# Four of the first modulation's sixteen maps taken as row sums on VectorE, the other twelve left on TensorE, and the first loads in a new order

## The chip, the cores and the metric

One core of one Trainium2 chip runs the whole program. The metric is device time in microseconds (us) of one execution. Engines are named as in the profile: PE is TensorE, PEld its weight loads, DVE VectorE, ACT ScalarE, POOL GpSimd, SP SyncE, which here only issues transfers.

## The reference, cut to what matters

A trunk of two layers works on 256 context tokens and 1024 latent tokens, 1024 features wide; layer 0 mixes tokens by a Conformer convolution module, layer 1 by grouped-query attention, and each is followed by a SwiGLU FFN. Only the first steps of layer 0 are touched by the change:

```python
silu_c, silu_cc = jax.nn.silu(c), jax.nn.silu(c_ctx)          # 1024 values each
mod_x = (silu_c  @ w_mod[i] + b_mod[i])[:, None, :]           # w_mod[i] is 1024 x 6144
mod_c =  silu_cc @ w_mod[i] + b_mod[i]
sh_x, sc_x, g_x, shf_x, scf_x, gf_x = jnp.split(mod_x, 6, axis=-1)
hx = rmsnorm(x,   norm_g[i, 0]) * (1.0 + sc_x) + sh_x
hc = rmsnorm(ctx, norm_g[i, 0]) * (1.0 + sc_c) + sh_c
yx, yc = conv_module(hx, ...), conv_module(hc, ...)           # begins with h @ w_pw1 (1024 x 2048)
```

So nothing of the first large matmul (pw1) can be completed before the first 2048 columns of the modulation, shift (sh) and scale (sc), are there: 16 blocks of 128 features, called maps here, numbers 0 to 7 for sh and 8 to 15 for sc.

## The kernel before, in words

Activations lie feature by token: 8 blocks k of 128 features on the partitions. The tokens are cut into three pieces: C (the 256 context tokens), L and R (512 latent tokens each). Every large matmul is made of three passes over a high and a low half of each operand (lines 450, 451 and 452 in `pw1`: high weights by high data, high by low, low by high).

`build` writes the work down in an order, and a scheduler turns it into one fixed queue of instructions for each engine, after data dependences and priorities. Each engine then works its queue strictly in order and waits by semaphores. The steps of the beginning are:

- `load_x` asks for the activations of a piece in four transfers (256 KB each for C, 512 KB for L and R), `load_map(i)` for one map of 512 KB, in the order map 0, map 8, map 1, map 9, and so on, into ten buffers. "The n-th map" below is the n-th in this order, counted from 0. All are issued by SP; a transfer is issued only once the one eight before it has landed.
- `mod_pe` computes one map on PE: eight matmuls (line 241) against both conditions at once give two rows of 128 values, ACT copies them (line 244), PE turns them upright (line 246), and ACT adds the bias (line 248). Two maps, sh and sc of the same block k, then let DVE make the scale column of block k (line 1095 before, 1128 after).
- `norm_in` is the RMS norm of a piece. ACT squares the eight blocks (lines 385 and 388), DVE adds them up (389), PE sums over the partitions (363), DVE takes the reciprocal root in some 12 dependent small instructions (341 to 368), PE spreads it (377). Then each block is applied: DVE multiplies (397), ACT adds the shift and rounds to the high half (402), DVE makes the low half (403). gC, gL and gR are the three pieces' norms, advanced in turn by `next`.
- `wload` loads a weight block of 512 KB into one of the two buffers wr0 and wr1 and splits it into a high half on ACT (143) and a low half on DVE (147). The first two blocks of pw1 are loaded in this way while the norms run.
- `cond_row` loads both conditions as one row repeated on all 128 partitions (1 MB, line 252) and takes their SiLU there (253). It serves `mod_dve`, which computes the later maps 16 to 39 on DVE during pw1: one dot product of a transposed map against a condition is one DVE instruction of 128 by 1024 and a small one that reads the accumulator (line 271).

PE's queue ends the beginning with pw1's block 0 on C and L, then the sums (363) and the spreading (377) of R's norm, then the second half of L and everything that follows.

Of the kernel before, what the change touches and what calls it, by code (L numbers as in the profile page):

```python
# [12 lines left out]
ALU = mybir.AluOpType  # L13
# [4 lines left out]
KT = D // P  # L18
# [36 lines left out]
class Kern:  # L55
# [1001 lines left out]
    def build(self):  # L1057
        nc, a, c = self.nc, self.a, None
        self.consts()
        c = self.c  # L1060
# [4 lines left out]
        cr = hr[:, TOK + nv:TOK + nv + 2048].rearrange("p (s d) -> p s d", s=2)  # L1065
        xs = {"C": hr[:, :KT * CTX].rearrange("p (k n) -> p k n", k=KT), "L": self.T("T6", [P, KT, 512])}

        def load_x(b):
            for q in range(0, KT, 2):
                nc.sync.dma_start(xs[b][:, q:q + 2, :], a["xT"][:, q:q + 2, PIECES[b][0]:PIECES[b][1]])  # L1070
        load_x("C")
        gC = self.norm_in(0, None, (None, "T1", "T1"), *PIECES["C"], hs["C"], xt=xs["C"])
        gL = self.norm_in(0, None, (None, "T2", "T3"), *PIECES["L"], hs["L"], xt=xs["L"])
        self.set_banks(mm=[0, 1, 2, 3], md=[4, 6], st=[4, 5, 6, 7])
# [4 lines left out]
        raws = [self.T(t, [P, 4, 1024]) for t in ("T4", "T5")] + [self.T("KB", [P, 2, 1024])]  # L1079
        raws = [raws[i][:, j] for j in range(4) for i in range(3) if j < raws[i].shape[1]]  # L1080

        def load_map(i):
            if i < 2 * KT:
                nc.sync.dma_start(raws[i % len(raws)], a["wmod"][i % 2 * KT + i // 2])
        for i in range(len(raws)):
            if i == 6:
                load_x("L")
            load_map(i)
        self.lo_dve = 1.0
        for k in range(KT):  # L1090
            for i in (2 * k, 2 * k + 1):
                self.mod_pe(i % 2 * KT + k, raws[i % len(raws)])
                load_map(i + len(raws))
            for s in range(2):
                nc.vector.scalar_tensor_tensor(out=self.col[0][s][0][:, k:k + 1], in0=self.mod[0][s][:, 8 + k:9 + k],
                                               scalar=1.0, in1=c["ng"][:, 0, 0, k:k + 1], op0=ALU.add, op1=ALU.mult)
            if k == 0:
                for _ in range(KT + 1):
                    next(gC)
            if k == 2:  # L1100
                for _ in range(KT + 1):
                    next(gL)
            next(gC)
            if k >= 2:
                next(gL)
            if k == 3:
                self.pre += [self.wload(a["pw1"][0]), self.wload(a["pw1"][KT])]
                xs["R"] = self.T("HS", [P, KT, 512])
                load_x("R")
                gR = self.norm_in(0, None, (None, "T4", "T5"), *PIECES["R"], hs["R"], xt=xs["R"])  # L1110
                self.cond_row(cr)
            if k > 3:
                for _ in range(3 if k < 6 else 2):
                    next(gR)
# [370 lines left out]
```

## Time and profile before

| | |
|---|---|
| median of 3 runs | 2964.86 us (2963.69 to 2965.74) |
| the profiled execution's own time | 2965.05 us |
| its span, first to last instruction | 2963.1 us |
| PE busy in the span | 2881.2 us, 97% |
| DVE busy | 1918.5 us, 65% |
| ACT busy | 1199.2 us, 40% |
| mean granted TensorE clock | 0.988 |

All times in the trace count from the first instruction of the span; 1.95 us of the execution's time lie outside it. A busy PE of 97% is an average over 3 ms: the change concerns only the first 70 us, which have to be read by themselves.

### The profile page before, as it was taken

The numbers are of one execution on the slowest core, as the hardware profiler recorded it, in microseconds if no ns is written. First come the engines' busy times: TensorE is split into PE (matmuls) and PEld (weight loads), VectorE is DVE, ScalarE is ACT, GpSimd is POOL, SyncE is SP. The second block draws the span as 40 slices with busy tenths as digits, with TensorE's granted clock in tenths as the row PEclk, the third lists the DMA queues.
The fourth block names the chain that finished last, engine by engine and source line by source line (L and its number), as shares of the span: only waits on it lengthen the run. The fifth ranks groups of instructions, "written<-read, shape, count | busy, mean of one in ns | idle before, by whom it ended". The sixth has DMA issues, their size and how long they took to land.

```text
span 2963.1 us, 38878 instructions
## 1 busy us (share of the span) xinstructions
PE 2881.2 (97%) x14914; PEld 2397.3 (81%) x14914; DVE 1918.5 (65%) x3340; ACT 1199.2 (40%) x1976; POOL 225.4 (8%) x381
## 2 busy tenths in 40 slices
PE   8999989999999999999999999989999999999997
PEld 5888877888888888888878777767777778888886
DVE  6887787847556368333577899786666657543335
ACT  5222265522222134222345788645555543332222
POOL 0000001011122011000011111100000000000000
PEclk9999999999999999999999999999999999999998
DMA  6443434334355234333355211322213143442332
GB/s 246 131 126 97 121 131 152 126 121 135 117 171 182 60 119 157 100 97 96 129 173 164 61 49 45 107 79 82 80 58 87 58 142 103 146 142 93 97 95 64
DMA packets 132138, 336.35 MB, mean 114 GB/s; under 512 B 31472, under 2 KB 53008, under 8 KB 130800
## 3 DMA queue, kind: packets, MB, share of 16 engines
q1 hardware_dynamic: 78624, 222.59, 23.3%
q0 software_dynamic: 29408, 103.83, 10.8%
q10 hardware_dynamic: 23920, 7.44, 1.1%
q8 instruction: 117, 1.92, 0.3%
q14 instruction: 69, 0.57, 0.1%
HBM read 289.50 MB, written 38.93 MB: 111 GB/s over the span
## 4 chain that ended last, share of the span: by engine, by line
PE 88%; DVE 7%; issue 2%; DMA 2%; ACT 1%; ACTq 0%; POOL 0%; SPq 0%; DVEq 0%; POOLq 0%
PE ps L171 21%; PE ps L172 21%; PE ps L173 21%; PE ps L982 4%; PE ps L1000 4%; PE ps L1006 2%; PE ps L1007 2%; PE ps L450 2%; PE ps L452 2%; PE ps L451 2%; PE ps L661 1%; PE ps L183 1%; PE ps L528 1%; PE ps L182 1%; PE ps L184 1%
## 5 line engine op out<-in xcount | busy, mean ns | idle before, releaser
L171 PE MATMUL ps<-T,wh 128*128 128x512 f32 (+1 forms) x2032 | 768.5, 378 | 0.5 <-DVE sm L804 0.4
L173 PE MATMUL ps<-T,wl 128*128 128x512 f32 (+1 forms) x2032 | 765.6, 377 | 3.0 <-DVE wl L147 3.0
L172 PE MATMUL ps<-T,wh 128*128 128x512 f32 (+1 forms) x1984 | 746.1, 376 | 0.0
L143 ACT CAST wh<-wr 128x1024 fp32r<-128x1024 f32 x285 | 299.3, 1050 | 737.4 <-PE ps L172 549.6
L147 DVE TENSOR_TENSOR wl<-wr,wh 128x1024 fp32r<-128x1024 f32 x285 | 348.4, 1223 | 291.4 <-ACT wh L143 286.6
L173 PEld LDWEIGHTS ps<-T,wl 128*128 128x128 f32 x2032 | 384.4, 189 | 73.1 <-DVE wl L147 3.7
L171 PEld LDWEIGHTS ps<-T,wh 128*128 128x128 f32 x2032 | 384.3, 189 | 69.8 <-ACT T L1345 1.7
L172 PEld LDWEIGHTS ps<-T,wh 128*128 128x128 f32 x1984 | 375.2, 189 | 66.4 <-DVE T L163 0.7
L172 PE MATMUL ps<-HS,wh 128*128 128x512 f32 (+1 forms) x768 | 297.7, 388 | 0.0
L1004 DVE TENSOR_TENSOR T<-ps,T 128x512 fp32r<-128x512 f32 x320 | 216.8, 687 | 108.1 <-ACT T L1003 107.3
L171 PE MATMUL ps<-HS,wh 128*128 128x512 f32 (+1 forms) x720 | 277.7, 388 | 0.0
L173 PE MATMUL ps<-HS,wl 128*128 128x512 f32 (+1 forms) x720 | 277.7, 386 | 0.0
L1003 ACT CAST T<-ps 128x512 fp32r<-128x512 f32 x320 | 185.9, 585 | 190.8 <-PE ps L1000 177.1
L1000 PE MATMUL ps<-cst,T 128*128 128x128 f32 x1100 | 189.3, 274 | 3.1 <-DVE T L1004 3.1
L988 DVE TENSOR_SCALAR_CACHE_REDUCE T<-ps,rq 128x1280 f32<-128x1280 f32 x110 | 170.0, 1546 | 28.0 <-PE ps L982 22.1
L835 DVE TENSOR_TENSOR T<-ps,T 128x512 f32<-128x512 f32 (+1 forms) x168 | 110.3, 662 | 116.2 <-PE ps L173 115.7
L1000 PEld LDWEIGHTS ps<-cst,T 128*128 128x128 f32 x1100 | 132.8, 141 | 49.3 <-DVE T L1004 30.6
L810 DVE TENSOR_TENSOR sm<-sm,ps 128x256 f32<-128x256 f32 (+1 forms) x88 | 54.5, 619 | 181.6 <-PE ps L173 181.5
L172 PEld LDWEIGHTS ps<-HS,wh 128*128 128x128 f32 x768 | 144.8, 188 | 27.6 <-DVE HS L163 0.2
L990 ACT ACTIVATE T<-T,mn 128x1280 f32<-128x1280 f32 x110 | 150.3, 1366 | 38.8 <-DVE T L988 38.4
L173 PEld LDWEIGHTS ps<-HS,wl 128*128 128x128 f32 x720 | 135.3, 188 | 26.9
L171 PEld LDWEIGHTS ps<-HS,wh 128*128 128x128 f32 x720 | 135.0, 188 | 26.2 <-ACT HS L160 0.8
(280 smaller groups left out, 4635.6 us busy)
## 6 DMA issues: line engine op xcount, KB each, us to landing
wr<-in_w SPq DMA_DIRECT2D x220, 512.0 KB, 3.5
q<-in_w SPq DMA_DIRECT2D x44, 512.0 KB, 3.4
wr<-in_pw SPq DMA_DIRECT2D x35, 512.0 KB, 3.5
HR<-in_wmodT POOLq DMA_DIRECT2D x56, 256.0 KB, 3.9
q<-in_wmodT POOLq DMA_DIRECT2D x56, 256.0 KB, 3.9
q<-qsd POOLq DMA_DIRECT2D x32, 256.0 KB, 3.3
wr<-in_wo SPq DMA_DIRECT2D x16, 512.0 KB, 3.5
qsd<-T POOLq DMA_DIRECT2D x14, 512.0 KB, 3.6
```

Of the source, the lines that this page charges most:

```text
L143: nc.scalar.copy(hi, raw)
L147: nc.vector.tensor_tensor(lo, raw, hi.bitcast(F32), op=ALU.subtract)
L171: nc.tensor.matmul(out[:, :n], lhsT=wh, rhs=xh, start=k == 0, stop=False)
L172: nc.tensor.matmul(out[:, :n], lhsT=wh, rhs=xl, start=False, stop=False)
L173: nc.tensor.matmul(out[:, :n], lhsT=wl, rhs=xh, start=False, stop=k == nk - 1)
L835: nc.vector.tensor_tensor(yd, out[:, :c1 - c0], yd, op=ALU.add)
L982: nc.tensor.matmul(sc[:, k0:k0 + w], lhsT=q[:, h, :], rhs=kt[:, p * TOK + k0:p * TOK + k0 + w], start=p == 0, stop=p == 1)
L988: nc.vector.tensor_scalar(out=pt, in0=sc, scalar1=rq[:, h:h + 1], scalar2=None, op0=ALU.mult, op1=ALU.min, accum_out=mn)
L990: nc.scalar.activation(pt, pt, AF.Exp, bias=mn, scale=-1.0, accum_out=sums[:, 0, h:h + 1])
L1000: nc.tensor.transpose(tp[:, h * P:(h + 1) * P], Ps[h][:, j * P:(j + 1) * P], c["ident"])
L1003: nc.scalar.copy(ph, tp)
L1004: nc.vector.tensor_tensor(pl, tp, ph.bitcast(F32), op=ALU.subtract)
```

## The change

Maps 6, 14, 7 and 15 (the sh and sc of blocks 6 and 7) leave PE. Their transposed form (`wmodT`, 512 KB each as well) is loaded, and DVE forms their eight dot products (`by_row`, line 1092) and adds the biases (line 1126). For this the conditions' row is loaded and its SiLU taken early instead of beside R. The first two maps are asked for ahead of the context tokens. Maps 6 and 15 go through the spare buffer q, maps 14 and 7 through wr1 and wr0, the buffers that pw1's first two weight blocks use next. The bytes that are loaded are the same.

```diff
-        load_x("C")
...
         def load_map(i):
-            if i < 2 * KT:
-                nc.sync.dma_start(raws[i % len(raws)], a["wmod"][i % 2 * KT + i // 2])
-        for i in range(len(raws)):
-            if i == 6:
-                load_x("L")
+            nc.sync.dma_start(raws[i % len(raws)], a["wmod"][i % 2 * KT + i // 2])
+
+        rows = [(f, self.raw() if i else self.room()) for i, f in enumerate((6, 14, 7))]
+        junk = self.ps[:, 2:4].rearrange("p a b -> p (a b)")
+
+        def load_row(f, raw):
+            nc.sync.dma_start(raw, a["wmodT"][0, f])
+
+        def by_row(f, raw):
+            for s in range(2):
+                nc.vector.tensor_tensor_reduce(out=junk, in0=raw, in1=cr[:, s, :], scale=1.0, scalar=0.0,
+                                               op0=ALU.mult, op1=ALU.add, accum_out=self.mod[0][s][:, f:f + 1])
+        for i in range(2):
             load_map(i)
+        load_x("C")
+        for i in (2, 3):
+            load_map(i)
+        self.cond_row(cr)
+        load_row(*rows[0])
+        for i in (4, 5):
+            load_map(i)
+        load_x("L")
+        load_map(6)
+        load_row(*rows[1])
+        load_map(7)
+        load_row(*rows[2])
+        for i in (8, 9):
+            load_map(i)
+        for row in rows:
+            by_row(*row)
+        rows.append((15, self.room()))
         self.lo_dve = 1.0
         for k in range(KT):
             for i in (2 * k, 2 * k + 1):
-                self.mod_pe(i % 2 * KT + k, raws[i % len(raws)])
-                load_map(i + len(raws))
+                if i < 12:
+                    self.mod_pe(i % 2 * KT + k, raws[i % len(raws)])
+                if i < 2:
+                    load_map(i + len(raws))
+                if i == 1:
+                    load_row(*rows[3])
+                    by_row(*rows[3])
+                    for s in range(2):
+                        for f in (6, 14):
+                            m = self.mod[0][s][:, f:f + 2]
+                            nc.vector.tensor_tensor(m, m, c["bmod"][:, 0, f:f + 2], op=ALU.add)
...
                 gR = self.norm_in(0, None, (None, "T4", "T5"), *PIECES["R"], hs["R"], xt=xs["R"])
-                self.cond_row(cr)
```

DVE's queue at the root of L's norm, before: sum (nv), root (nq, nh, nr) and the first application to L (sb<-T6) stand nearly together.

```order
L368 TENSOR_SCALAR nv_296<-ps_72 128x4
L341 TENSOR_SCALAR nq_304<-nv_296 128x4
L345 TENSOR_SCALAR nh_303<-nv_296 128x4
L343 TENSOR_SCALAR nr_302<-nq_304 128x4
L347 TENSOR_TENSOR nq_304<-nr_302 128x4
L403 SCALAR_TENSOR_TENSOR T1_204<-sb_321,mod01_102,T1_204 128x256
L348 TENSOR_TENSOR nq_304<-nq_304,nh_303 128x4
```

The same place after the change; the instructions that read wr1 and wr0 are the dot products of maps 14 and 7.

```order
L1092 ISA ps_72,mod00_101<-wr1_74,HR_105 128x1024
L1092 ISA mod00_101 128x1
L368 TENSOR_SCALAR nv_312<-ps_72 128x4
L1092 ISA ps_72,mod01_102<-wr1_74,HR_105 128x1024
L1092 ISA mod01_102 128x1
L341 TENSOR_SCALAR nq_320<-nv_312 128x4
L345 TENSOR_SCALAR nh_319<-nv_312 128x4
L343 TENSOR_SCALAR nr_318<-nq_320 128x4
L347 TENSOR_TENSOR nq_320<-nr_318 128x4
L348 TENSOR_TENSOR nq_320<-nq_320,nh_319 128x4
L349 SCALAR_TENSOR_TENSOR nr_318<-nq_320,nr_318 128x4
L1092 ISA ps_72,mod00_101<-wr0_73,HR_105 128x1024
```

Two dots of map 14 stand ahead of the root and two of map 7 inside it (the second of these a few rows on); before, none did.

PE's queue where L's root is spread (line 377), before: the sixth and seventh map are just done, and eight maps are still to come.

```order
L246 MATMUL ps_72<-cst_75,sm_339 128x2
L377 MATMUL ps_72<-cst_75,nr_302 128x128 x4
L246 MATMUL ps_72<-cst_75,sm_352 128x2
L241 MATMUL ps_72<-T4_113,cs_99 2x128 x8
L241 MATMUL ps_72<-T5_114,cs_99 2x128 x8
```

After the change, the same place in PE's queue:

```order
L246 MATMUL ps_72<-cst_75,sm_368 128x2
L241 MATMUL ps_72<-T4_109,cs_99 2x128 x8
L377 MATMUL ps_72<-cst_75,nr_318 128x128 x4
L241 MATMUL ps_72<-T5_110,cs_99 2x128 x8
L246 MATMUL ps_72<-cst_75,sm_406 128x2
L241 MATMUL ps_72<-T4_109,cs_99 2x128 x5
L246 MATMUL ps_72<-cst_75,sm_419 128x2
L241 MATMUL ps_72<-T4_109,cs_99 2x128 x3
L241 MATMUL ps_72<-T5_110,cs_99 2x128 x8
```

The spreading now stands between map 8 and map 9, and maps 9, 10 and 11, the last three on PE, are queued behind it.

DVE's queue after the scale columns (line 1095, 1128) of block 4, before: C and L are applied and the two low halves of pw1's weights follow (L147).

```order
L1095 SCALAR_TENSOR_TENSOR col010_112<-mod01_102,cst_75 128x1
L397 SCALAR_TENSOR_TENSOR sb_412<-HR_105,col010_112,ps_72 128x256
L397 SCALAR_TENSOR_TENSOR sb_416<-T6_106,col000_111,ps_72 128x512
L403 SCALAR_TENSOR_TENSOR T1_204<-sb_412,mod01_102,T1_204 128x256
L403 SCALAR_TENSOR_TENSOR T3_326<-sb_416,mod00_101,T2_325 128x512
```

After the change, the dots of map 15 (buffer q) stand there:

```order
L1128 SCALAR_TENSOR_TENSOR col010_108<-mod01_102,cst_75 128x1
L1092 ISA ps_72,mod00_101<-q_142,HR_105 128x1024
L1092 ISA mod00_101 128x1
L397 SCALAR_TENSOR_TENSOR sb_426<-HR_105,col010_108,ps_72 128x256
L1092 ISA ps_72,mod01_102<-q_142,HR_105 128x1024
L1092 ISA mod01_102 128x1
L1126 TENSOR_TENSOR mod00_101<-mod00_101,cst_75 128x2
L147 TENSOR_TENSOR wl_384<-wr1_74,wh_383 128x1024
```

pw1's first low half now follows the dots of map 15. Up to the spreading of R's root (line 377 again) PE's queue holds the same pw1 matmuls in both kernels, 48 of 256 columns and 18 of 512.

## Rows read from the trace of the kernel before

**Rows 1.** Busy time of each engine by stretch of the span: stretch, its length, busy us and instructions of PE, PEld, DVE, ACT and POOL, granted clock, DMA share, GB/s.

```profile
0.00:50.00 50.00, 37.44 (x290) 26.20 (x291) 24.59 (x74) 24.73 (x74) 0.20 (x4) 1.00 0.88 331
50.00:100.00 50.00, 47.62 (x242) 39.40 (x241) 42.34 (x80) 23.69 (x38) 0.20 (x3) 0.93 0.32 93
100.00:500.00 400.00, 382.91 (x2089) 334.45 (x2088) 326.22 (x593) 134.86 (x246) 10.45 (x17) 0.98 0.42 123
```

**Rows 2.** Instructions of PE in order of time: start, us from the first start to the last end, engine, line, tile, shape, count, and idle time before them with what ended it. The first two maps together, one later map, the last upright turn (line 246) ahead of pw1, and the first matmul of pw1's unbroken run. A map's eight matmuls are 16 entries here.

```profile
9.49 6.20 PE L241 MATMUL ps<-T,cs 128*2 128x128 f32 x32 [9.49 <-DMA T<-in_wmod]
42.01 1.91 PE L241 MATMUL ps<-KB,cs 128*2 128x128 f32 x16
50.23 0.22 PE L246 MATMUL ps<-cst,sm 2*128 2x2 f32 x1
50.38 0.38 PE L452 MATMUL ps<-T,wl 128*128 128x256 f32 x1
```

**Rows 3.** Issues of SP in order of time (start, us): the eleventh map, the thirteenth map, the last transfer of R, the conditions' row. Counted in portions of 512 KB they are number 17, 19 and 28, and the row 29 and 30.

```profile
17.23 0.33 SPq L1084 DMA_DIRECT2D T<-in_wmod  x1
19.93 0.33 SPq L1084 DMA_DIRECT2D KB<-in_wmod  x1
31.43 0.37 SPq L1070 DMA_DIRECT2D HS<-in_xT  x1
32.72 0.34 SPq L252 DMA_DIRECT2D HR<-in_crow  x1
```

**Rows 4.** The same four transfers in the list of issues, each asked for in a narrow stretch around its issue: size, and us from issue to landing.

```profile
T<-in_wmod SPq DMA_DIRECT2D x1, 512.0 KB, 10.3
KB<-in_wmod SPq DMA_DIRECT2D x1, 512.0 KB, 10.2
HS<-in_xT SPq DMA_DIRECT2D x1, 512.0 KB, 10.5
HR<-in_crow SPq DMA_DIRECT2D x1, 1024.0 KB, 13.2
```

**Rows 5.** DVE's busy time (and instructions) in two stretches, with granted clock, DMA share and GB/s.

```profile
42.20:49.30 7.10, 2.90 (x6) 1.00 0.30 96
33.30:64.30 31.00, 23.41 (x56) 0.97 0.55 189
```

**Rows 6.** What DVE waited for between 33.3 and 64.3 us: us in total, times, longest.

```profile
DVE wl L147 <- ACT wh L143: 3.6, 2, 2.6
DVE col L1095 <- ACT mod L248: 2.1, 2, 1.3
DVE sb L397 <- PE ps L377: 0.7, 1, 0.7
DVE acc L389 <- ACT sb L388: 0.6, 1, 0.6
```

**Rows 7.** DVE in order of time: the first application of L's norm, the first sum of R's squares, R's root from its first to its last step, and the first application of R's norm.

```profile
33.36 0.75 DVE L397 SCALAR_TENSOR_TENSOR sb<-T,col,ps 128x512 f32<-128x512 f32 x1 [0.74 <-PE ps L377]
49.33 0.69 DVE L389 TENSOR_TENSOR acc<-acc,sb 128x512 f32<-128x512 f32 x1 [0.59 <-ACT sb L388]
62.11 0.16 DVE L341 TENSOR_SCALAR nq<-nv 128x4 int32<-128x4 int32 x1
63.10 0.16 DVE L347 TENSOR_TENSOR nq<-nr 128x4 f32<-128x4 f32 x1
64.08 0.16 DVE L349 SCALAR_TENSOR_TENSOR nr<-nq,nr 128x4 f32<-128x4 f32 x1
65.46 0.75 DVE L397 SCALAR_TENSOR_TENSOR sb<-HS,col,ps 128x512 f32<-128x512 f32 x1 [0.81 <-PE ps L377]
```

**Rows 8.** DVE in order of time during pw1: two dot products of 1024 values on 128 partitions, and the reading of the first one's accumulator.

```profile
104.69 1.23 DVE L271 CUSTOM_DVE_ANT_0 ps<-KB,HR 128x1024 f32<-128x1024 f32 x1
105.83 0.14 DVE L271 DVE_READ_ACCUMULATOR2_ANT mod<- 128x1 f32 x1
106.01 1.23 DVE L271 CUSTOM_DVE_ANT_0 ps<-KB,HR 128x1024 f32<-128x1024 f32 x1
```

**Rows 9.** PE in order of time around R's norm: the sums of its squares, the spreading of its root, and a pass of 512 columns shortly behind it and one later.

```profile
58.84 0.95 PE L363 MATMUL ps<-cst,acc 128*128 128x1 f32 x8
64.31 1.11 PE L377 MATMUL ps<-cst,nr 128*128 128x128 f32 x4 [1.04 <-DVE nr L349]
66.07 0.63 PE L452 MATMUL ps<-T,wl 128*128 128x512 f32 x1
69.42 0.40 PE L451 MATMUL ps<-T,wh 128*128 128x512 f32 x1
```

**Rows 10.** PE's busy time (and matmuls) in stretches of 2 us, with the granted clock, DMA share and GB/s.

```profile
60.00:62.00 2.00, 1.27 (x6) 1.00 0.00 0
62.00:64.00 2.00, 1.26 (x5) 0.63 0.86 260
66.00:68.00 2.00, 2.00 (x6) 0.50 0.29 41
68.00:70.00 2.00, 2.00 (x7) 0.66 0.18 25
70.00:72.00 2.00, 2.00 (x11) 1.00 0.00 0
```

**Rows 11.** Two of ACT's instructions in order of time: the SiLU of the conditions' row, and the first square of R.

```profile
56.54 1.91 ACT L253 ACTIVATE HR<-HR 128x2048 f32<-128x2048 f32 x1
48.15 0.63 ACT L385 ACTIVATE acc<-HS 128x512 f32<-128x512 f32 x1
```

**Rows 12.** One of PE's waits between 100 and 560 us, at the context piece's second projection.

```profile
PE ps L661 <- ACT T L642: 1.1, 1, 1.1
```

## Prediction, made before the changed kernel was run

> **What bounds the beginning now.** I first read the busy times by stretch, since 97% over 3 ms says nothing of 70 us [rows 1]. In the first 50 us PE is busy for 37.4, DVE for about half of the time, and the transfers take 0.88 of the DMA engines: here three resources compete. From 100 us on PE is busy for 383 of 400 us, and there only a change of PE's own work would count.
>
> Then PE in order of time [rows 2]. Its maps run from 9.49 to 50.45 us. Sixteen maps in 41 us are 2.56 us each: 1.91 for the matmuls, the rest turns and waits. The transfers don't set this pace. Two maps that were asked for as portions 17 and 19 of 512 KB [rows 3] were there after 10.3 and 10.2 us [rows 4], at 27.5 and 30.1; the last part of R, portion 28, was there at 41.9. That is (41.9 - 27.5) / 11 = 1.31 us a portion, twice as fast as PE takes maps. So PE is behind, and only DVE has room: between 42.2 and 49.3 it works 2.9 of 7.1 us [rows 5].
>
> Taking four maps off PE saves it 4 x 2.56 = 10.2 us. Whether the end sees this depends on what comes behind the maps. DVE adds R's squares from 49.33 and ends the root at 64.24 [rows 7]. PE then waits 1.04 us for just that before it spreads the root at 64.31 [rows 9]. So the last wait of the beginning is on DVE, not on PE. From 33.3 to 64.3 DVE works 23.41 of 31.0 us [rows 5]; of its 7.6 idle us, 7.0 stand in four waits [rows 6], for ACT's high halves (3.6), for scale columns that wait on PE's maps (2.1), for the spreading of L's root (0.7), for R's squares (0.6). Behind the spreading PE is full in each stretch [rows 10]. Up to there its queue holds the same pw1 matmuls in both kernels. The change in the whole time is thus taken as the shift of the end of R's root, plus what the clock gives or takes behind it.
>
> **The parts.** *PE's maps:* minus 10.2 us, worth this only if DVE keeps up.
>
> *The dot products.* During pw1 one dot takes 1.23 us and the next starts 1.32 after it [rows 8]; that one is an instruction of the same shape. Eight are 10.6 us of DVE. Those of map 6 lie ahead of L's norm, where DVE waits for loads. The others:
>
> 1. Map 14 is portion 17 of the new order and map 7 portion 19, so they land where portions 17 and 19 landed before, at 27.5 and 30.1. The conditions' row, 1 MB, is counted as two portions, 2.6 us. Before, it landed at 45.9, 4.0 after R [rows 3, 4]; if that is its price in the crowd too, everything behind it is 1.4 us late. I take 2.6: at the old place few other transfers were left to fill the queue.
> 2. L is portions 12 to 15 and is summed by about 27. Dot, sum nv, dot of map 14: from 27.7 to 30.5. The first half of the root, whose steps took 62.11 to 63.10 in R [rows 7], is done at 31.5. Two dots of map 7, interleaved with single steps of 0.2: 34.3. Second half of the root with two scale columns between: 35.6. PE spreads it at once (its map 8 is done by then), and the first application of L starts 0.75 behind, at 36.4. Before it was at 33.36 [rows 7]. **L's norm is 3.0 us later.**
> 3. From there to the end of R's root DVE has the old work, 23.4 us, and the two dots of map 15 with their additions, 2.64 + 0.3: 26.3 us.
> 4. Waits in this stretch. The maps end near 44 rather than 50.4, so the scale columns (2.1 us of waits) come free, R's squares (ACT, 48.15 before [rows 11]) and the high halves (3.6) have time to get ahead of a DVE that is late. I keep 0.9 of the old 7.6: 0.6 for three maps that now stand on PE behind L's spreading and 0.3 for single steps. Bounds: 0 and, if the later pair of high halves (2.6 of the 3.6) still waits for a buffer, 2.6.
> 5. R's root ends at 36.4 + 26.3 + 0.9 = 63.6, against 64.24: **minus 0.6 us.**
>
> *ACT's SiLU of the row,* 1.91 us, leaves 56.54 [rows 11] for about 16 us, where ACT has 24.7 busy us of 50 [rows 1]: nothing. It took ACT's time beside R then; since DVE was the later of the two, no gain is counted either (bound 1.9).
>
> *wr1 and wr0* are held until the dots of maps 14 and 7 are done, 30.5 and 34.3. As pw1's blocks are portions 25 and 26, landing at about 38 and 39, SP's issues behind them wait at most for a buffer that is free before. R follows; its 2 MB are there by 45, ahead of its first sum at about 47.6. Nothing, unless the dots slip by more than 3 us.
>
> *The clock.* Before, PE had gaps between 60 and 64 and the granted clock was 0.63, then 0.50 and 0.66 in stretches that PE filled, up to 69.3 [rows 10]; a pass of 512 columns took 0.63 there and 0.40 behind it [rows 9]. About 4.2 us at 1.2 GHz rather than 2.4 cost 2.1 us. With the maps gone early the gaps ahead of R's spreading do not get fewer, so I keep the 2.1: change nothing, bounds minus 2.1 and plus 2.1 (the low level lasting twice as long).
>
> *Later stages* have the same order but for swapped neighbours. The widest wait that such a swap touches is 1.1 us [rows 12]: 0, bounds plus and minus 1.
>
> Sum: the profiled execution took 2965.05 (span 2963.1 and 1.95 outside), 0.19 over the median. 2965.05 - 0.6 = **2964.4**.
>
> **A rule against the change.** At its start PE waits for loads between maps, and the first two maps took 6.20 us rather than 2 x 1.91 = 3.82 [rows 2]; from 60 to 62 PE is busy for 1.27 of 2 us and the clock is 1.00, a stretch later 0.63 [rows 10]. So gaps have cost clock here, and by the same rows not every gap has. The Trainium skill, TensorE: Matmul & The Clock Gate, section "HAM oscillation — how this bites in real kernels", says that where PE waits for a transfer between bursts, each burst starts cold again. By that the twelve maps, now paced by loads with rows, L and C between them, would run at half speed again and again; the trace before, where PE was always behind its loads, cannot show it. This is rival C; the sum without it is 2964.4, with it the figure given there.
>
> **Rivals.**
>
> *A, the forecast:* DVE takes over as the bound, and what PE saves is spent in DVE's queue. For it: 26.3 us of work behind a start that hangs on two late loads. 2964.4, own range 2962.5 to 2967.
>
> *B1:* the waits vanish (-0.9), and PE, whose pw1 work ahead of R is then closer to R's root, keeps its clock (-2.1): 2961.4. For it: DVE idles least in the whole stretch; against it: the gaps of [rows 10] are made by the same root.
>
> *B2:* PE's saving comes through, 2965.05 - 10.2 = 2954.9. It needs DVE to have 10 us less to do between L and R than I count, so dots that cost far less than [rows 8], or landings far ahead of 1.31 us a portion, with the dots of maps 14 and 7 inside DVE's waits. Half of that would give 2960.
>
> *C, slower:* PE falls to its lower level in the gaps of the load-paced beginning. A map's matmuls then take about 1.2 us more (6.20 - 3.82, halved) up to 1.9 more (half speed). The map that stands half on either side of L's spreading and the next, both at half speed, are 3.1 us more ahead of the scale columns of blocks 4 and 5, for which DVE waits. With the row's 1.4 us: 2964.4 + 4.5 = 2968.9. It counts as slower by over 0.2% from 2970.8 on, so from another 1.9 us, one more map at half speed on the path.
>
> *D, nothing changes:* DVE hides everything and R's sums stay at 49.33, held by ACT: 2965, not told apart from A by the time.
>
> **Chances.** A with D 0.58, B1 0.14, B2 or half of it 0.10, C 0.18. The likeliest gives 2964.4. Leaving out the far half of B2 and the far half of C, the range is 2957.5 to 2969.5. 0.2% (5.9 us) is about what a measurement of this kernel can tell from no change, so faster begins below 2958.9: most of B2 and a rest of B1 in which several bounds add up (-0.9, -2.1, -1 and -1.9), 0.15. Slower begins above 2970.8: half of C, 0.09. Within: 0.76.
>
> **What would show it.** Right: first application of L at about 36.4; DVE idle for at most 1.5 us from there to R's root; first sum of R near 47.6; R spread on PE near 63.7 after a wait for DVE's root; granted clock near 0.5 for some 4 us behind. Step 1 is wrong if map 14 or 7 lands elsewhere than 27.5 and 30.1, step 2 if L's application is not 3 us late, step 4 if DVE still waits for columns or high halves. B shows as R's spreading far below 63, or as a clock of 1.00 from 64 to 70. C shows as granted clock under 1 between 15 and 45 us with maps of over 1.91 us, and as DVE waiting for scale columns. The forecast also fails if some stage behind 100 us, where only swapped neighbours differ, moves by more than 1 us.

## The result, and the profile after

| | before | after |
|---|---|---|
| median | 2964.84 us (20 runs, 2961.57 to 2970.25) | 2974.26 us (20 runs, 2969.11 to 2977.92) |
| ratio | | 1.0028, 95% interval 1.0022 to 1.0035 |
| profiled execution | 2965.05 us | 2969.64 us |

The change made the kernel slower by 0.28%, about 8 to 9 us. Forecast was 2964.4, range 2957.5 to 2969.5: wrong. The profiled execution of after is among the fastest of its twenty, so its trace shows only half of the loss; this matters below. Of the runs of before that were taken beside the experiments, one took 10081 us; it is left out of all means below.

Busy time by stretch, as in [rows 1]:

```profile
0.00:50.00 50.00, 34.11 (x235) 23.18 (x236) 31.10 (x86) 22.65 (x65) 0.40 (x7) 0.90 0.88 322
50.00:100.00 50.00, 47.01 (x232) 38.95 (x231) 47.14 (x91) 23.70 (x36) 0.00 (x0) 0.93 0.38 119
100.00:500.00 400.00, 381.79 (x2085) 333.34 (x2085) 323.36 (x588) 134.69 (x246) 10.25 (x16) 0.98 0.41 121
```

PE is busy for only 3.3 us less in the first 50 us, though four maps of 1.91 us and their turns are gone: part of the difference is pw1, which begins sooner, and part a granted clock of 0.90 instead of 1.00. DVE has 6.5 us more there and 4.8 more in the next 50.

DVE in order of time: the first dot of map 6; the first and the last sum of L's squares; the sum nv, a scale column inside L's root and the last step of that root; the first application of L; then the first sum of R's squares, the last step of R's root and the first application of R [rows 7].

```profile
19.30 1.23 DVE L1092 CUSTOM_DVE_ANT_0 ps<-q,HR 128x1024 f32<-128x1024 f32 x1 [2.12 <-ACT HR L253]
24.08 0.69 DVE L389 TENSOR_TENSOR acc<-acc,sb 128x512 f32<-128x512 f32 x1 [0.71 <-ACT sb L388]
29.50 0.68 DVE L389 TENSOR_TENSOR acc<-acc,sb 128x512 f32<-128x512 f32 x1
32.21 0.16 DVE L368 TENSOR_SCALAR nv<-ps 128x4 f32<-128x4 f32 x1 [0.81 <-PE ps L363]
37.86 0.16 DVE L1128 SCALAR_TENSOR_TENSOR col<-mod,cst 128x1 f32<-128x1 f32 x1 [0.75 <-ACT mod L248]
38.52 0.16 DVE L349 SCALAR_TENSOR_TENSOR nr<-nq,nr 128x4 f32<-128x4 f32 x1
40.15 0.75 DVE L397 SCALAR_TENSOR_TENSOR sb<-T,col,ps 128x512 f32<-128x512 f32 x1 [1.47 <-PE ps L377]
51.00 0.69 DVE L389 TENSOR_TENSOR acc<-acc,sb 128x512 f32<-128x512 f32 x1 [0.21 <-ACT sb L388]
65.82 0.16 DVE L349 SCALAR_TENSOR_TENSOR nr<-nq,nr 128x4 f32<-128x4 f32 x1
67.02 0.75 DVE L397 SCALAR_TENSOR_TENSOR sb<-HS,col,ps 128x512 f32<-128x512 f32 x1 [0.64 <-PE ps L377]
```

L is applied 6.8 us later than before (40.15 against 33.36), not 3.0. Behind that DVE is nearly without a gap, as forecast: its busy time from 40.1 to 66 is 24.76 of 25.9 us.

```profile
40.10:66.00 25.90, 22.20 (x127) 16.56 (x126) 24.76 (x60) 17.42 (x36) 0.00 (x0) 0.88 0.47 165
```

PE in order of time: the first two maps; a later map, an upright turn and the first part of another map, each with a gap ahead; the sums of L's squares, in the middle of that map; the rest of it and the next one; map 8 and L's spreading; the last upright turn; R's spreading [rows 9]. Then two instructions of ACT: the SiLU of the conditions' row and the biases behind it. Then PE's busy time and granted clock (behind POOL's column) in five stretches.

```profile
5.75 5.05 PE L241 MATMUL ps<-T,cs 128*2 128x128 f32 x32 [5.75 <-ACT cs L228]
19.61 1.91 PE L241 MATMUL ps<-T,cs 128*2 128x128 f32 x16 [1.88 <-ACT mod L248]
24.54 0.22 PE L246 MATMUL ps<-cst,sm 2*128 2x2 f32 x1 [1.13 <-ACT sm L244]
26.47 1.44 PE L241 MATMUL ps<-T,cs 128*2 128x128 f32 x6 [1.72 <-DMA T<-in_wmod]
30.34 1.84 PE L363 MATMUL ps<-cst,acc 128*128 128x1 f32 x8 [2.42 <-DVE acc L389]
32.10 4.86 PE L241 MATMUL ps<-T,cs 128*2 128x128 f32 x26
37.62 1.91 PE L241 MATMUL ps<-T,cs 128*2 128x128 f32 x16
39.46 0.65 PE L377 MATMUL ps<-cst,nr 128*128 128x128 f32 x4
49.26 0.22 PE L246 MATMUL ps<-cst,sm 2*128 2x2 f32 x1
66.04 0.94 PE L377 MATMUL ps<-cst,nr 128*128 128x128 f32 x4 [0.28 <-DVE nr L349]
```

```profile
17.36 1.90 ACT L253 ACTIVATE HR<-HR 128x2048 f32<-128x2048 f32 x1
19.18 0.67 ACT L248 ACTIVATE mod<-ps,cst 128x1 f32<-128x1 f32 x4
```

```profile
26.00:28.00 2.00, 1.44 (x6) 0.60 (x6) 1.79 (x3) 1.90 (x4) 0.00 (x0) 0.50 1.03 412
28.00:36.00 8.00, 5.67 (x27) 4.12 (x28) 7.07 (x20) 0.76 (x2) 0.00 (x0) 0.50 0.99 379
60.00:66.00 6.00, 5.73 (x19) 4.68 (x19) 5.69 (x21) 3.08 (x5) 0.00 (x0) 0.50 0.27 87
66.00:68.00 2.00, 1.96 (x10) 1.75 (x11) 1.36 (x3) 0.18 (x1) 0.00 (x0) 0.83 0.05 8
68.00:70.00 2.00, 2.00 (x10) 1.66 (x9) 2.00 (x4) 1.84 (x3) 0.00 (x0) 1.00 0.30 42
```

Two things to see. From 26 to 36 us PE runs at 1.2 GHz, after gaps of 1.9, 1.1 and 1.7 us and around one of 2.4; rival C's clock came true. But only the gap of 1.7 us ended with a load. The first ended with ACT, where the row's SiLU stands ahead of the biases that PE waited for, the second with ACT too, and the last with DVE's sums of L's squares. In all seven traces with the new beginning the first and the last are there (1.9, and 2.4 to 4.8 us). And around R the lower level has moved: before it lay mostly behind the spreading, from 62 to 69 us [rows 10], now it lies ahead of it, so that PE is back at 2.4 GHz soon after 66. In this execution that gives back what the 1.7 us later spreading costs.

### The profile page after: what moved, and what is told of

Its sections match the earlier page's. It is cut to its first block, busy times and chain, and to the rows that moved or that the text cites. A ratio compares the mean times of both kernels' runs of the same rounds, so it can differ in the third digit from the quotient of the medians.

```text
span 2967.6 us, 38745 instructions
## 1 busy us (share of the span) xinstructions
PE 2879.8 (97%) x14846; PEld 2395.9 (81%) x14846; DVE 1928.0 (65%) x3360; ACT 1197.4 (40%) x1964; POOL 226.0 (8%) x381
## 4 chain that ended last, share of the span: by engine, by line
PE 88%; DVE 7%; DMA 2%; issue 2%; ACT 1%; ACTq 0%; POOL 0%; DVEq 0%; SPq 0%; POOLq 0%
PE ps L171 21%; PE ps L172 20%; PE ps L173 20%; PE ps L982 4%; PE ps L1000 4%; PE ps L1006 2%; PE ps L1007 2%; PE ps L450 2%; PE ps L452 2%; PE ps L451 2%; PE ps L528 1%; PE ps L183 1%; PE ps L182 1%; PE ps L184 1%; PE ps L661 1%
## 5 line engine op out<-in xcount | busy, mean ns | idle before, releaser
L147 DVE TENSOR_TENSOR wl<-wr,wh 128x1024 fp32r<-128x1024 f32 x287 | 350.9, 1223 | 283.5 <-ACT wh L143 279.4
L988 DVE TENSOR_SCALAR_CACHE_REDUCE T<-ps,rq 128x1280 f32<-128x1280 f32 x110 | 170.1, 1546 | 27.5 <-PE ps L982 22.1
```

The source lines that it names most:

```text
L147: nc.vector.tensor_tensor(lo, raw, hi.bitcast(F32), op=ALU.subtract)
L988: nc.vector.tensor_scalar(out=pt, in0=sc, scalar1=rq[:, h:h + 1], scalar2=None, op0=ALU.mult, op1=ALU.min, accum_out=mn)
```

## The experiments

Means below are over all runs of a kernel, with the standard error. The kernel before, over 114 runs beside the experiments, has 2965.6 +- 0.2; the changed one 2974.0 +- 0.4 over 26.

### Two causes or one

The order of instructions after the beginning shows one more effect of the change that the diff hides. `raw()` counts up an index over the weight buffers; the two rows that take wr1 and wr0 move it by two. With two buffers that changes nothing, but from the second projection on there are three (wr0, wr1, q), and then each later weight block lands in another buffer than before. One line sets the count back, or moves it in the kernel before:

```diff
-        rows.append((15, self.room()))
+        rows.append((15, self.room())); self.ri -= 2
```

```diff
-        self.lo_dve = 1.0
+        self.lo_dve, self.ri = 1.0, self.ri + 2
```

The first is `a_ring`, made from after, the second `b_ring`, made from before.

`a_again` and `b_again` are the two kernels unchanged, for second traces.

> The changed kernel once more, for a second trace and more times. In the first trace R's root is spread 1.7 us later than before, the clock behind it recovers sooner, and from 145 to 360 us the changed kernel is 0.7 us ahead; at 1140 us it stands level, at 1520 us 2.4 behind, at the end 4.5. Theory A (the beginning costs it): the second trace loses its time before 150 us. Theory B (the turn of the weight buffers): it loses it again at 1180 to 1520 and 1560 to 1860 us. Theory C (chance of the clock): the places of the loss differ from the first trace. All: about 2969 to 2978 us.

> The kernel before once more, for a second trace and as a control. Ratio 1.000, 2961 to 2970 us. Theory C: the stretches at the lower clock behind 370 us differ in number from the first trace by as much as they do between the two kernels; theories A and B: they stand at the same places and have the same lengths within one step.

> The changed kernel, with the count of weight buffers set back by the two buffers that the rows took, so that every later weight block goes to the buffer (wr0, wr1 or q) that it has in the kernel before. The beginning is the changed one. Theory B: the loss goes, 2964 us, and from 1140 us on no further loss. Theories A and C: still 2974.

> The kernel before, with the count of weight buffers moved on by two, so that only the later turn of wr0, wr1 and q is that of the changed kernel. Theory B: 2970 to 2974 us. Theories A and C: 2965, as before.

Medians: `a_again` 2975.0 (ratio 1.0030, interval 1.0019 to 1.0042), `b_again` 2966.49 (0.9999, 0.9990 to 1.0008), `a_ring` 2969.47 (1.0012, 1.0003 to 1.0020), `b_ring` 2967.74 (1.0006, 0.9997 to 1.0015). So theory A (the beginning) and theory B (the buffers' turn) each hold a part, and neither alone.

In the new beginning, the scratch buffer q is also reserved earlier, which moves the scratch buffers within SBUF. The next pair tells whether that counts, and gives second estimates:

```diff
-        raws = [raws[i][:, j] for j in range(4) for i in range(3) if j < raws[i].shape[1]]
+        raws = [raws[i][:, j] for j in range(4) for i in range(3) if j < raws[i].shape[1]]; self.room()
```

This, in the kernel before, is `b_addr`, and in `b_ring` it is `b_both`. `a_addr` is `a_ring` with the scratch buffers sm, acc, sb and four tiny ones reserved at the same line, ahead of q, as they lie in before.

> The kernel before with one line that reserves the spare buffer q ahead of the small scratch buffers, as the changed kernel does. The order of all instructions on every engine is that of the kernel before; only the places of q, sm, acc, sb and four tiny buffers within SBUF are those of the changed kernel. Behind the beginning, the changed kernel with the weight buffers set back has the very instructions of before, yet was 4 us slower in the median while the cut kernels differ by only 1. Theory P (the places in SBUF cost it): 2968 to 2969 us. Theory H (the beginning costs it, by the clock or otherwise) and theory C (chance): 2965.5.

> The kernel before with both: the count of weight buffers moved on by two and q reserved early. From pw1 on this is the changed kernel, instruction by instruction and place by place; only the beginning is that of before. Whatever it takes over 2965.5 us is the price of what the change does to the later stages, and what the changed kernel (2974) takes over this is the price of the beginning. Theory P: 2971 to 2974. Theory H: 2968, as with the count alone.

> The changed kernel with both undone: the weight buffers set back and the scratch buffers reserved in the old order, so that from pw1 on it is the kernel before, place by place, and only the beginning is changed. Theory P: 2965 to 2967. Theory H: 2969 to 2970, as with the count alone.

Medians: `b_addr` 2965.11 (1.0000, 0.9991 to 1.0009), `b_both` 2967.32 (1.0012, 1.0003 to 1.0020), `a_addr` 2969.89 (1.0015, 1.0006 to 1.0024). The places in SBUF cost nothing: theory P is out. Taken together:

| beginning | weight buffers as before | weight buffers moved on |
|---|---|---|
| old | 2965.6 +- 0.2 | 2967.7 +- 0.5 (`b_ring`, `b_both`, 22 runs) |
| new | 2969.5 +- 0.5 (`a_ring`, `a_addr`, 22 runs) | 2974.0 +- 0.4 (after, `a_again`) |

The buffers' turn costs 2.1 us with the old beginning and 4.5 with the new; the new beginning costs 3.9 with the old turn or 6.3 with the new. The two don't simply add.

**Where the buffers cost.** PE's waits from 1562 to 1590 us, in after (us in total, times, longest):

```profile
PE ps L886 <- ACT sm L879: 0.6, 1, 0.6
```

`a_again` (0.6), `b_ring` (0.7) and `b_both` (0.7) have this wait; before, `b_again`, `b_addr`, `a_ring` and `a_addr` don't. In `a_again` it is seen between two passes of the FFN:

```profile
1570.57 0.40 PE L171 MATMUL ps<-T,wh 128*128 128x512 f32 x1
1571.57 0.38 PE L886 MATMUL ps<-cst,sm 128*128 128x4 f32 x2 [0.60 <-ACT sm L879]
```

Some 300 us on, PE's longest wait between 1860 and 1885 us is 2.5 us in after (2.4 in `a_again`) and 1.4 before:

```profile
PE ps L1006 <- ACT T L1003: 2.5, 1, 2.5
```

But this wait goes with the turn only beside the new beginning: it is 1.2 in `b_ring` and 0.7 in `b_both`, which have the moved turn, and up to 1.8 in `a_addr`, which has the old one.

The time between two fixed points shows the price better than single waits. They are PE's wait for ACT ahead of the second FFN part and its wait for DVE at a norm; here in before, then in `b_both`:

```profile
1514.38 0.73 PE L182 MATMUL ps<-T,wh 128*128 128x512 f32 x2 [1.53 <-ACT T L402]
1952.81 1.12 PE L731 MATMUL ps<-cst,nr 128*128 128x128 f32 x4 [5.52 <-DVE nr L349]
```

```profile
1515.40 0.74 PE L182 MATMUL ps<-T,wh 128*128 128x512 f32 x2 [1.52 <-ACT T L402]
1957.63 1.11 PE L731 MATMUL ps<-cst,nr 128*128 128x128 f32 x4 [5.50 <-DVE nr L349]
```

That is 438.4 and 442.2 us. Over the traces with the old turn (before, `b_again`, `b_addr`, `a_ring`, `a_addr`) it is 438.4 to 441.1, mean 439.6; with the moved one (after, `a_again`, `b_ring`, `b_both`) 440.1 to 445.9, mean 443.2. The four whole kernels of the next sections keep the old turn too; with them it has 438.4 to 441.3, mean 440.0, so single traces of the two kinds overlap. The first wait itself is 0.6 us. In `a_again`, `b_ring` and `b_both` a short stretch at 1.2 GHz stands beside that wait, here in `b_both` as a granted clock of 0.91, where before has 1.00:

```profile
1560.00:1580.00 20.00, 19.31 (x88) 15.83 (x87) 12.15 (x25) 7.71 (x12) 1.44 (x2) 0.91 0.38 129
```

### The beginning

A trace is one execution, and here that misleads. PE's spreading of R's root (line 377) by trace:

| beginning | starts at, us | mean |
|---|---|---|
| old, 10 traces | 64.31, 64.83, 63.38, 62.83, 63.34, 63.81, 63.39, 63.24, 63.14, 62.94 | 63.5 |
| new, 7 traces | 66.04, 68.07, 67.47, 66.81, 68.22, 67.41, 67.87 | 67.4 |
| new, PE kept busy, 2 traces | 65.53, 65.26 | 65.4 |
| old, only the order of loads, 1 trace | 65.45 | |

The two traces that I compared first are a late one of the old kind and the earliest of the new kind: 1.7 us apart, where the kinds are 3.9 apart. In `a_again`:

```profile
68.07 1.04 PE L377 MATMUL ps<-cst,nr 128*128 128x128 f32 x4 [0.29 <-DVE nr L349]
```

**Does the lower clock in the beginning cost it?** `a_warm` is `a_addr` with four maps' matmuls made twice:

```diff
-            for k in range(KT):
+            for k in [*range(KT)] * self.again:
...
-                    self.mod_pe(i % 2 * KT + k, raws[i % len(raws)])
+                    self.again = 1 + (2 <= i < 6); self.mod_pe(i % 2 * KT + k, raws[i % len(raws)])
```

> The last kernel, with the matmuls of the third to the sixth map made twice (the second time gives the result), so that TensorE has less idle time between 13 and 28 us; this adds some 7 us of its work there. Theory W (the stretch at the lower clock from 26 to 36 us, with maps that take 4.9 instead of 3.8 us, delays L's norm): granted clock 1.00 up to 36 us, the first application of L at 39 us or sooner instead of 40.2, total the same or up to 1 us less. If the lower clock there costs the end nothing: the same total within 0.5 us, or more by what the added matmuls delay.

PE's stretches from 13 to 25 and 25 to 37 us in `a_addr`, then in `a_warm`:

```profile
13.00:25.00 12.00, 9.65 (x68) 6.19 (x65) 6.58 (x21) 5.35 (x13) 0.20 (x3) 0.86 1.03 396
25.00:37.00 12.00, 6.78 (x36) 4.78 (x37) 9.88 (x25) 4.59 (x13) 0.00 (x0) 0.72 0.92 359
```

```profile
13.00:25.00 12.00, 11.62 (x101) 8.52 (x102) 7.13 (x25) 5.10 (x11) 0.00 (x0) 1.00 1.02 395
25.00:37.00 12.00, 10.46 (x90) 7.61 (x88) 9.87 (x26) 6.07 (x19) 0.20 (x3) 1.00 0.90 344
```

The clock stays at 1.00 although PE has more to do, R's spreading comes 2.0 us sooner, and the whole takes 2967.1 +- 0.6 (ratio to before 1.0010, 1.0001 to 1.0019): 2.4 +- 0.7 us less than `a_ring` and `a_addr`. So somewhat over half of the beginning's price goes with the lower clock among the maps. The rest, 1.5 us in the time and 1.9 at the spreading, stays with the clock full. DVE's longer queue is one candidate for it, but the next run shows another.

**The order of loads alone.** `h_ord` only asks for maps 0 and 8 ahead of the context tokens:

```diff
-        load_x("C")
...
+            if i == 2:
+                load_x("C")
```

> The kernel before with one part of the change alone: the first two maps are asked for ahead of the context tokens; all sixteen maps stay on TensorE, the conditions' row stays late, and behind the beginning nothing differs. TensorE's maps begin at about 5.8 instead of 9.5 us. If TensorE's maps set the time of the beginning: up to 3.7 us faster, 2962. If VectorE's queue up to R's root sets it: R's root ends at most 1 us sooner, 2964 to 2966. If gaps between the first maps lower the clock as in the changed kernel: 2966 to 2969.

2967.31 in the median, mean 2967.0 +- 0.3 (ratio 1.0003, 0.9994 to 1.0012): the maps begin at 5.83 instead of 9.49, and nothing is gained; by the means 1.4 us are lost (0.9 +- 0.5 against the 15 runs of before taken beside it). R is spread at 65.45, later than in each trace of the old kind, after a wait of 0.8 for DVE. Starting PE sooner doesn't start DVE sooner: L is applied at 33.52 against 33.36. And the order of loads alone, with no dot in DVE's queue ahead of R, comes out as late as `a_warm`, at the spreading and about so in the time. Whether the rest that `a_warm` leaves is DVE's queue or this order is not told apart. No version tried beats the kernel before.

### Where in the program the beginning's price is paid

`b_cut` and `a_cut` end behind pw1, `b_mid` and `a_mid` behind the first FFN (both repeated as `b_mid2`, `a_mid2`, and `w_mid` is the busy-PE variant ended there).

> The kernel before, ended behind pw1: it leaves out everything from the end of pw1 on and writes the gated half of pw1 eight times as output, so it takes some 310 us and shows the beginning alone. It is the base for the next kernel; only the difference of the two counts. Theory A (the beginning costs the time) and theory D (the beginning costs nothing; the time is lost behind pw1) say the same of it.

> The changed kernel, ended in the same way behind pw1 (it leaves out everything from there on). In three traces each, the instructions at 240 us stand 0.7, 0.5 and 2.0 us ahead of the first trace of before with the new beginning, and 0, 0.8 and 1.3 ahead with the old one. Theory D: level with the other cut kernel within 1 us, or up to 1 us faster. Theory A: 4 us slower, as the whole kernel with the weight buffers set back was in the median.

> The kernel before, ended behind the first FFN at about 1510 us: it leaves out everything after it (the second part of layer 0 and all of layer 1) and writes that FFN's result twice as output. It is the base for the next kernel; only the difference of the two counts.

> The changed kernel with the weight buffers and the scratch places of before, ended in the same way (everything behind the first FFN is left out). The full pair of this kind differed by 4.1 us over 22 and 112 runs, the pair cut behind pw1 by 0.6 with an uncertainty of 1. Theory H (the beginning costs it at once): 4 us slower. Theory T (with the same instructions behind, the loss comes at the later waits, by the clock): 0 to 1.5 us slower.

> The kernel before, ended behind the first FFN, once more (it leaves out all that follows): base for the next two, to halve the uncertainty of the difference, which was 1.6 us with an uncertainty of 0.9 over 4 runs each. 1089.4.

> The changed beginning with the later stages of before, ended in the same way (all behind the first FFN is left out), once more. Theory H (the beginning costs the 4 us at once): 1093. Theory T (1 us or so in the beginning, the rest at the later waits): 1090 to 1091.

> The same with the matmuls of four early maps made twice, so that TensorE stays at the higher clock in the beginning, ended in the same way (all behind the first FFN is left out). In the whole kernel this took 2.4 us less than without. If those 2.4 us are saved in the beginning: 1088 to 1089, 2 us under the kernel without them. If they are saved later: level with it within 0.7 us.

Behind pw1: 361.72 and 362.82 in the median; means 0.6 +- 1.0 apart. Behind the FFN, both pairs together, 8 runs each: 1088.7 +- 0.6 and 1091.0 +- 0.4, 2.3 +- 0.7 apart. In the whole kernel 3.9 +- 0.5. `w_mid` has 1090.9 +- 0.4, level with `a_mid`, so the 2.4 us that it saves in the whole kernel don't show at that point. I had expected a price that is paid by 100 us and stays.

The traces agree with the pair behind pw1. At fixed points (those with matmuls added to pw1 left out) R's spreading is 3.9 us later with the new beginning, but PE's first matmul of line 529, near 113 us, only 2.2: the lower clock now lies ahead of the spreading, so that the ten matmuls behind it take 1.7 us less. At PE's wait of [rows 12] it is 0.6 +- 0.6 (means 387.0 of seven traces and 387.6 of six); here in before, then in `a_again`:

```profile
387.79 2.93 PE L661 MATMUL ps<-T,wr 128*128 128x256 f32 x6 [1.11 <-ACT T L642]
388.13 2.93 PE L661 MATMUL ps<-T,wr 128*128 128x256 f32 x6 [1.11 <-ACT T L642]
```

At the wait near 1514 us it is 0.8 +- 0.9 (five traces and four). So the 3.9 us at the spreading and the 3.9 us in the whole time are the same figure by chance; most of the first is given back within pw1.

Three explanations were tested or weighed: the instructions behind the beginning are, in `a_ring` and `a_addr`, the same and in the same order as before from about 105 us on; their places in SBUF count nothing (above); and a mere shift costs only its length, as two delays show, four (`b_d4`, below) or eight (`b_d8`) matmuls more in a gapless part of pw1:

```diff
+                    for _ in range(4 * (k == 4 and b == "R" and o is pa and i == 0)):
+                        nc.tensor.matmul(o[:, :n], lhsT=wh, rhs=xh[:, i], start=True, stop=True)
```

> The kernel before with four matmuls of 512 columns more in the middle of pw1 (the first one of a group made five times), where TensorE works without a gap: at 0.23 us each everything behind is 0.9 us later, and nothing else differs. Theory U (a shift of the later stages costs what it is long): 0.9 us over before, 2966.2. Theory L (where the later stages' waits fall against the steps of the clock decides, and the start of the program does not fall on them evenly): away from +0.9 by some us in either direction, with the mean granted clock moved by 0.001 to 0.002.

> The same with eight matmuls: 1.8 us. Theory U: 2967.1 and the granted clock of before. Theory L: away from +1.8 by some us, the clock moved.

2965.9 +- 0.5 and 2967.1 +- 0.7, that is 0.3 and 1.5 over before for shifts of 0.9 and 1.8: theory U. How the 3.9 us divide between the first 100 us and the later waits **stays open**: the differences of the cut pairs lie some three and two standard errors below 3.9, and the mean granted clock (0.9871 before, 0.9846 for `a_ring` and `a_addr`, so by estimate some 15 us more at the lower level, of which the trace of after has 10 in the beginning; `a_warm` has 0.9872) suggests that part of it is a stretch more at 1.2 GHz later on.

## Why the prediction was wrong, step by step

**Right.** What bounds the beginning: DVE's queue up to R's root, not PE; PE waits there for DVE in every trace (0.6 to 1.3 us with the old beginning, 0.3 with the new), and a PE that starts 3.7 us sooner gains nothing. Step 1, the landings: asked for at 16.00 and 18.57, 11.7 us each to land, 27.7 and 30.3 against the forecast 27.5 and 30.1.

```profile
16.00 0.34 SPq L1088 DMA_DIRECT2D wr<-in_wmodT  x1
18.57 0.33 SPq L1088 DMA_DIRECT2D wr<-in_wmodT  x1
```

Dots of 1.23 us, as in [rows 8]. Steps 3 and 4: from L's application to R's root 26.3 + 0.9 were forecast; 25.8 were measured, of them 24.8 busy: the waits about as forecast, the work 1.5 less. The waits for high halves of [rows 6] did go, and those for scale columns fell from 2.1 to 0.4.

**Wrong, step 2 (L's norm 3.0 us later).** It was 6.8. I let L's squares be summed "by about 27"; the last sum ended at 30.2. That was a guess from L's landing, not from DVE's queue: there the dots of map 6 stand ahead of these sums, and they waited 2.1 us for ACT's SiLU of the row, which itself stood in ACT's queue behind the maps' copies. "Ahead of L's norm, where DVE waits for loads" put 2.6 us of dots and this wait at nothing. So the edit that I costed at nothing, the early SiLU, was late for the first instruction that needed it, and it held up PE for 1.9 us as well, the first of the gaps above. Then the sums on PE took 1.84 instead of 0.95 at the lower clock [rows 9], a scale column inside the root was waited for 0.75, and the spreading was waited for 1.5 instead of 0.7 [rows 6]: map 8, which I had done by then, kept PE until 39.5.

**Wrong, in step 4, that the maps end near 44 rather than 50.4.** The last upright turn ended at 49.5. What PE saved on four maps went into its waits for ACT and DVE and into 10 us at the lower clock.

**Wrong, step 5 (R's root 0.6 us sooner).** It ended at 65.98 in the trace, 2.4 later than forecast; over the traces R's spreading is 3.9 later than in the old kind. The base was off too: the profiled execution of before is 0.8 later at this point than the mean of its kind.

**Wrong, the later stages (0, bounds plus and minus 1).** This term was mis-sized most plainly: the turn of three weight buffers cost 2.1 to 4.5 us. I read the later differences as swapped neighbours and priced them by one wait of 1.1 [rows 12]. What moved them was a counter, and the place was 1500 us behind the change.

**Rival C** named the clock rightly, though not what would hold PE up: PE's gaps brought the clock to 0.50 for 10 us, and a PE kept busy kept it at 1.00. The rule of the Trainium skill that was weighed (TensorE: Matmul & The Clock Gate, "HAM oscillation — how this bites in real kernels") agrees in kind, since idle time between bursts cost clock; but three of the four gaps ended with ACT or DVE and not with a transfer, and the clock fell once among the maps, not at each burst. One row that C was drawn from had been misread: the first two maps of [rows 2] hold no gap, their first 24 entries start 0.21 us apart and the last eight 0.11, at a granted clock that reads 1.00. C's price, 4.5 us, was worked out for scale columns, which waited 0.75 us inside L's root and 0.4 behind it; what it held up was L's sums. The busy PE saved 2.4. That and the buffers' 4.5 are 6.9 of the 8.4 us between the means; the other 1.5 have no shown cause. I had treated every loss outside the beginning as a rest.

## What to carry to other kernels

When a change takes a buffer or an index from a shared ring, follow that ring to the end of the program: the price can lie far behind the edit, and one line that sets the index back tells it apart. An engine that is relieved gains nothing while another's queue sets the pace; and work put "into the idle time" of an in-order queue is free only if its inputs are there first, so look for what each new instruction stands ahead of. For effects of a few us, compare several traces of each kind at one fixed point before trusting two.

## What the runs showed that I had not expected

The same kernel, run after run, spans some 8 us (2961 to 2969 for most runs before, a spread of about 2 us around the mean), and the time of R's spreading varies by 2 us between traces of one instruction order. A wait of TensorE can be followed by a stretch at 1.2 GHz, whose length differs between executions of one kernel: around the same wait of 1.5 us near 1514 us, the granted clock from 1500 to 1520 us was 0.83 in before and 0.74 in `b_again`.
